# Feature sums of the norms in chained groups of four, modulation sums in chained pairs

## The chip, the cores and the metric

The kernel runs on one core of one Trainium2 chip. A core has engines that run side by side, each through its own queue in order: PE (matrix products, with a separate row PEld for the loading of weights), DVE, ACT and POOL (element-wise work), and SP, which issues most DMAs. The metric is device time in microseconds for one execution; lower is better. The time before is 3664.76 us, the median of three runs (3664.4 to 3665.83).

## The reference

Two post-norm layers over 1024 latent tokens and 256 context tokens of 1024 features, in float32. A layer modulates its input by vectors that come from a conditioning vector, projects it, runs three kinds of attention heads side by side, projects back, adds a gated residual and normalises; then a gated feed-forward with the same residual form. Cut to what the change touches:

```python
mod = (silu_c @ w_ada[l] + b_ada[l])[:, None, :]      # and the same for the context
sh1, sc1, g1, sh2, sc2, g2 = jnp.split(mod, 6, axis=-1)
x = layer_norm(DEEPNORM_ALPHA * x + g1 * (o @ w_out[l]), ln1_g[l], ln1_b[l])
x = layer_norm(DEEPNORM_ALPHA * x + g2 * swiglu(modulate(x, sh2, sc2), w_ffn_in[l], w_ffn_out[l]), ln2_g[l], ln2_b[l])

def layer_norm(x, g, b):
    mu = jnp.mean(x, axis=-1, keepdims=True)
    var = jnp.mean(jnp.square(x - mu), axis=-1, keepdims=True)
    return (x - mu) * lax.rsqrt(var + LN_EPS) * g + b
```

The context's stream goes through the same norms in the first layer only.

## The kernel before

Activations lie with features on the 128 partitions and tokens along the free axis, so 1024 features are eight tiles (`KT` = 8) of up to 1280 tokens. Tokens go in chunks of 512, 512 and, in the first layer, 256 (context). A projection (`mm3`, L278) is done in three PE passes on fp32r operands: weights and activations are split into a high and a low part (`whi` by ACT in L249, `wlo` mostly by POOL in L252), and hi·hi, hi·lo and lo·hi are added up in one PSUM bank. With eight feature tiles that is 24 products of 128x128 by 128x512 for 128 output features of one chunk. Each finished block of the output projection or of the feed-forward is added to the residual tile `z[kt]` by one DVE instruction (`ev_res`, L1198).

When all eight tiles of a chunk are there, `layer_norm` sums over the features. A sum over partitions is done on PE, by a product with a 128x32 tile of ones: `fsum` (L360 to L368) gives tile kt to the column quarter kt % 4 of PE, so that four partial sums stand on four blocks of 32 partitions of one PSUM bank, and tiles 4 to 7 are added onto those of 0 to 3. These are full fp32 products, which PE runs as two instructions each. ACT copies the bank out, another product brings the four quarters together and spreads the mean (L384). Then the mean is subtracted (tiles 0 to 3 on DVE, 4 to 7 on POOL; in the last norms 3 tiles on POOL), ACT squares each tile into a buffer `lnsq` (L395), `fsum` sums the squares, a few products and DVE steps give the reciprocal root, and the tiles are scaled and handed on: modulated and split for the next projection, scaled by the norm's own weights (POOL, L374), and stored. The buffers of the squares, of the mean's copy, of the bank's copy and of the modulated tiles are one pool of five (`t512`). There are ten such chunk norms: three and three in the first layer, two and two in the second, and each has two `fsum`, of eight products each.

While one chunk's norm runs, PE works at the projections of the next chunk, and the norm's products stand among them in PE's queue.

The conditioning vectors of the next parts are made beside the feed-forward and the projections: `ada_step` multiplies a 128x512 block of `w_ada` by the two conditioning columns on DVE (L177, L179), adds up eight such blocks in two accumulators, one for each column, and then two products with ones on two column quarters (L185) sum them over the partitions. Twenty such pairs are made.

The order of each engine's queue isn't the program's: a planner lays out all instructions when the kernel is built, by its own estimate of when each can start and by the order in which the program gives them. The kernel steers it with `gate(ins, after)`, an edge that only says that one instruction is issued after another, and `in_order`, which chains a list with such edges. Neither says that nothing else may come between. The sums of the softmax (`inverse_sums`, L498) and the spread of their inverses (`along`, L508) are chained in this way already. For the first norm of a layer, `hook` ties the 6th, 13th, 53rd, 58th and 73rd full-width projection product behind five steps of the norm: the last product of the first sum, the mean's, the last product of the second sum, the variance's and the root's.

Of the kernel before, what the change touches and what calls it, by code (L numbers as in the profile page):

```python
# [12 lines left out]
AF = mybir.ActivationFunctionType  # L13
ALU = mybir.AluOpType
# [8 lines left out]
KT = 8  # L23
# [30 lines left out]
def body(ctx: ExitStack, tc, xT, cT, w_ada, w_in, nbias, wa2, w_out, w_fi, w_fo, vecs, cc, consts, ropes, gmask, out):  # L54
    nc = tc.nc
    act, dve, pool, pe = nc.scalar, nc.vector, nc.gpsimd, nc.tensor
# [19 lines left out]
    def t512(name="t5"):  # L76
        return tmp.tile([P, 512], F32, tag="t5", name=name)
# [4 lines left out]
    def bank_x(name):  # L82
        return ps_x.tile([P, 512], F32, tag="x", name=name)

    def bank_a(name):
        return ps_a.tile([P, 512], F32, tag="a", name=name)
# [20 lines left out]
    ones = const.tile([P, 32], F32, name="ones")  # L107
# [10 lines left out]
    scc = const.tile([P, KT, 32], F32, name="scc")  # L118
# [21 lines left out]
    def ada_end(l, streams, ps, sel):  # L140
        sb = t512("adasb")
        act.copy(sb, ps)
        pv = bank_x("adav")
        for m in range(4):
            pe.matmul(pv[:, 4 * m:4 * m + 4], lhsT=sb[:, m * P:(m + 1) * P], rhs=sel, start=True, stop=True)
        for i, (part, half) in enumerate(streams):
            c0 = V_BADA + part * KT + half * 4
            dve.tensor_tensor(
                out=mod[l][:, part, half * 4:half * 4 + 4, :],
                in0=pv[:, 0:16].rearrange("p (m s) -> p m s", s=4)[:, :, 2 * i:2 * i + 2],  # L150
                in1=vec[l][:, c0:c0 + 4].unsqueeze(2).to_broadcast([P, 4, 2]), op=ALU.add)
# [13 lines left out]
    ada_todo, ada_run, ada_st = [], [], {}  # L165
# [6 lines left out]
    def ada_step(l, st, i, k, raw):  # L172
        if k == 0:
            ada_st["acc"] = [spool.tile([P, 512], F32, tag="hl", name="adacc") for _ in range(2)]
        for s_, a in enumerate(ada_st["acc"]):
            if k == 0:
                dve.tensor_scalar(a, raw, scc[:, k, s_:s_ + 1], None, ALU.mult)  # L177
            else:
                dve.scalar_tensor_tensor(out=a, in0=raw, scalar=scc[:, k, s_:s_ + 1], in1=a, op0=ALU.mult, op1=ALU.add)  # L179
        if k == KT - 1:  # L180
            if i == 0:
                ada_st["ps"] = bank_a("adaps")
            for s_, a in enumerate(ada_st["acc"]):
                q = 2 * i + s_
                pe.matmul(ada_st["ps"][32 * q:32 * q + 32, :], lhsT=ones[:, 0:32], rhs=a, start=True, stop=True)  # L185
            if i == 1:
                ada_end(l, st, ada_st["ps"], ident[:, 0:P:32])

# [115 lines left out]
    def hook(products_, offs):  # L304
        hk["c"] = 0
        hooks[:] = zip(offs, products_)
# [38 lines left out]
    def rsqrt_cols(src, n, eps, rows=P):  # L345
        v = small.tile([P, 20], F32, tag="rq_v", name="rq_v", bufs=2)
        y = small.tile([P, 20], F32, tag="rq_y", name="rq_y", bufs=2)
        t = small.tile([P, 20], F32, tag="rq_t", name="rq_t", bufs=2)
        v, y, t = v[:rows, :n], y[:rows, :n], t[:rows, :n]
        dve.tensor_scalar(v, src, eps, None, ALU.add)  # L350

        dve.tensor_scalar(y.bitcast(I32), v.bitcast(I32), -0.5, 1597463007.0, ALU.mult, ALU.add)
        for _ in range(3):
            dve.tensor_tensor(out=t, in0=y, in1=y, op=ALU.mult)
            dve.scalar_tensor_tensor(out=t, in0=t, scalar=-0.5, in1=v, op0=ALU.mult, op1=ALU.mult)
            dve.scalar_tensor_tensor(out=y, in0=t, scalar=1.5, in1=y, op0=ALU.add, op1=ALU.mult)
        return y


    def fsum(src, n):  # L360

        ps = bank_x("fs")
        for kt in range(KT):
            q = kt % 4
            ins = pe.matmul(ps[32 * q:32 * q + 32, :n], lhsT=ones[:, 0:32], rhs=src(kt), start=(kt < 4), stop=(kt >= 4))  # L365
        sb = t512("fssb")
        act.copy(sb[:, :n], ps[:, :n])
        return sb, ins  # L368
# [6 lines left out]

    NPOOL = 4
    NP3 = 3

    def layer_norm(z, t0, n, eps, consume, npool=NPOOL, offs=None):
        sl = slice(t0, t0 + n)  # L380
        nb = n // P
        sb, x1 = fsum(lambda kt: z[kt][:, sl], n)
        mps = bank_x("mean")
        x2 = pe.matmul(mps[:, :n], lhsT=onesm, rhs=sb[:, :n], start=True, stop=True)  # L384
        msb = t512("meansb")
        act.copy(msb[:, :n], mps[:, :n])
        for kt in range(KT):
            if kt >= KT - npool:
                pool.tensor_tensor(out=z[kt][:, sl], in0=z[kt][:, sl], in1=msb[:, :n], op=ALU.subtract)
            else:  # L390
                dve.tensor_tensor(out=z[kt][:, sl], in0=z[kt][:, sl], in1=mps[:, :n], op=ALU.subtract)

        def sq(kt):
            q = t512("lnsq")
            act.activation(q[:, :n], z[kt][:, sl], AF.Square)  # L395
            return q[:, :n]

        sb, x3 = fsum(sq, n)
        vps = bank_x("var")
        for b in range(nb):  # L400
            x4 = pe.matmul(vps[:, b:b + 1], lhsT=sb[:, b * P:(b + 1) * P], rhs=ones1, start=True, stop=True)
        y = rsqrt_cols(vps[:, :nb], nb, eps)
        rps = bank_x("rstd")
        for b in range(nb):
            x5 = pe.matmul(rps[:, b * P:(b + 1) * P], lhsT=y[:, b:b + 1].to_broadcast([P, P]), rhs=ident,
                           start=True, stop=True)
        if offs and n == 512:
            hook((x1, x2, x3, x4, x5), offs)
        rsb = t512("rstdsb")
        act.copy(rsb[:, :n], rps[:, :n])  # L410
        for kt in range(KT):
            if kt >= KT - npool:
                pool.tensor_tensor(out=z[kt][:, sl], in0=z[kt][:, sl], in1=rsb[:, :n], op=ALU.mult)
            else:
                dve.tensor_tensor(out=z[kt][:, sl], in0=z[kt][:, sl], in1=rps[:, :n], op=ALU.mult)
            consume(kt, sl)
# [24 lines left out]
    def gate(ins, after):  # L441

        if after is not None:
            tc.add_manual_dep(ins.ins, after.ins.name, NOSYNC, reason="buffers in order of use")
        return ins

    def in_order(inss):

        for a, b in zip(inss, inss[1:]):
            gate(b, a)  # L450
        return inss[-1]
# [80 lines left out]
    for l in range(NL):  # L532
# [35 lines left out]
        for e in range(2):  # L568
            ba = V[:, V_BA + e:V_BA + e + 1]
            for (t0, n) in FULL:  # L570
                ps = bank_q("zps")
# [4 lines left out]
        ins = [act.activation(a, a, AF.Exp, scale=-1.0) for a in dec][-1]  # L576
        ins = [gate(act.activation(a, a, AF.Ln, bias=one1), ins) for a in dec][-1]
# [45 lines left out]
        for p, ga, gb in abanks:  # L623
            dst, src, n = a_mm(p, ga, gb, gk, gq)
# [6 lines left out]
        for lev in range(6):  # L631
# [8 lines left out]
            for p, ga, gb in abanks:  # L640
                dst, src, n = a_mm(p, ga, gb, xk_, X)
# [81 lines left out]
        for p in range(2):  # L723
# [5 lines left out]
            for par in range(2):  # L729
                for g0, g1 in ((0, 8), (8, 10)):  # L730
                    pt = bank_q("inc")
                    for g in range(g0, g1):
                        for e in range(2):
                            for hh in range(2):
                                h, r0 = 2 * p + hh, 64 * e + 32 * hh
                                pe.matmul(pt[r0:r0 + 32, (g - g0) * 64:(g - g0 + 1) * 64],
                                          lhsT=kdt[e][64 * par:64 * par + 64, g * P + 32 * h:g * P + 32 * h + 32],
                                          rhs=vg(g)[64 * par:64 * par + 64, h * 64:(h + 1) * 64], start=True, stop=True)
# [13 lines left out]
            for i in range(1, NCH - 1):  # L752
                for e in range(2):
                    c, nx = order[e][i], order[e][i + 1]
# [3 lines left out]
                                             op0=ALU.mult, op1=ALU.add)  # L758
# [377 lines left out]
        sb = {"n": 0, "t": ps_s.tile([P, 2, 2, 512], F32, tag="s4", name="sT", bufs=1)}  # L1136
# [11 lines left out]
        for x, i in enumerate(PAIRS):  # L1148
            if x < 5:
                load(PAIRS[x + 1])  # L1150
            if x in (0, 2):
# [3 lines left out]
            a, na, places, skip = (  # L1155
                (some(PAIRS[1], None), steps_a[3], 22, 2), (), (some(PAIRS[3], None), steps_a[3] - half, 22, 2), (),
                (some(PAIRS[5], None), steps_a[3] - half, 22, 2), (iter(()), 0, 39, 0))[x] or (
                chain(some(PAIRS[x + 2], half), some(PAIRS[x + 1], None)), half + steps_a[0], 39, 3)
            live, tails = tails, []
            b = stage_b(i)  # L1160
            n = done = 0
# [22 lines left out]
        z = []  # L1184
# [9 lines left out]
        def ev_res(g, m):  # L1194
            def ev(ps, t0, n, c):
                s = 0 if t0 < SEQ else 1
                zz = z[m + c][:, t0:t0 + n]
                dve.scalar_tensor_tensor(out=zz, in0=ps[:, :n], scalar=g[:, m + c, s:s + 1], in1=zz,  # L1198
                                         op0=ALU.mult, op1=ALU.add)
            return ev  # L1200

        groups = GROUPS[l]
# [7 lines left out]
        for grp in groups:  # L1210
            for m in range(0 if grp[0][0] >= SEQ else 2, KT):
                dense(w_out[l, :, m * P:(m + 1) * P], oh_all, ol_all, grp, ev_res(ga1, m))
            for (t0, n) in grp:
                def consume(kt, sl, t0=t0, n=n):
                    modulate(u2h, u2l, z[kt][:, sl], kt, l, 1, t0, n, dve)
                    affine(AFF1, z[kt][:, sl], aGB[:, 0, kt:kt + 1], aGB[:, 1, kt:kt + 1])
# [51 lines left out]
        for grp in GROUPS[l]:  # L1268
# [4 lines left out]
            for (t0, n) in grp:  # L1273
                def consume2(kt, sl, t0=t0, n=n):
# [6 lines left out]
                    elif t0 < SEQ:  # L1281
                        nc.sync.dma_start(xs[kt * P:(kt + 1) * P, sl], z[kt][:, sl])
                layer_norm(z, t0, n, LN_EPS, consume2, NP3 if last else NPOOL)

# [99 lines left out]
```

## Time and profile before

| what | value |
|---|---|
| median of three runs | 3664.76 us (3664.4 to 3665.83) |
| the profiled execution's own time | 3658.13 us |
| its span, first to last instruction | 3656.3 us |
| PE busy | 3406.7 us, 93% |
| DVE, POOL, ACT busy | 1640.7, 1150.5, 920.8 us |
| mean granted clock of PE | 0.962 |
| products of `fsum` | 320 PE instructions |
| products of `ada_step` | 80 PE instructions |

A row of the timeline gives the start in us, the length in us, the engine, the line, the operation, output and inputs, the shape, and after x how many like instructions in a row were merged into it; in brackets stands idle time of the engine just before, and what ended it. Busy time of overlapping instructions is counted once. PE's products are pipelined, so that a product's length is more than its distance from the next one's start. Some matmul records can be missing.

### The profile page before, as it was taken

What the parts mean: (1) busy time and instruction counts of PE and PEld (TensorE: products, weight loads), DVE (VectorE), ACT (ScalarE), POOL (GpSimd) and SP (SyncE); (2) the same over time, 40 slices, a digit from 0 to 9 for tenths busy, and PEclk for the clock granted to TensorE, in tenths of its full rate; (3) what the DMA queues carried; (4) which work ended last, traced back from release to release, by engine and by line L of the source; (5) the groups of instructions that cost most, each with busy time, mean ns of one, the idle gap of its engine ahead of it and who ended that gap; (6) DMA issues with size and microseconds to landing.
All of it is one profiled execution on the core that took longest, in us unless ns stands there. A gap on an engine that the chain in (4) does not pass through costs nothing. (4 is left out here: it accounts for less than half of the span.)

```text
span 3656.3 us, 49289 instructions
## 1 busy us (share of the span) xinstructions
PE 3406.7 (93%) x20832; PEld 2519.1 (69%) x20832; DVE 1640.7 (45%) x2535; ACT 920.8 (25%) x1365; POOL 1150.5 (31%) x687
## 2 busy tenths in 40 slices
PE   6798987889999999999999988998889999999998
PEld 3576773434678888888886577773335688888875
DVE  2757725553444554554135473426552532222233
ACT  2213212333231111111113413212332311111114
POOL 1212214664451111111125521315662622222223
PEclk8798998999999999999999998998999999999999
DMA  5253330102221222222123221220103111111122
GB/s 173 62 153 96 127 118 28 64 1 81 70 61 63 92 86 72 78 84 67 37 68 98 77 87 56 73 104 32 58 1 107 46 50 52 47 52 48 48 73 86
DMA packets 287277, 262.94 MB, mean 72 GB/s; under 512 B 13840, under 2 KB 238416, under 8 KB 287056
## 3 DMA queue, kind: packets, MB, share of 16 engines
q1 hardware_dynamic: 287056, 259.80, 22.2%
q8 instruction: 163, 2.67, 0.3%
q14 instruction: 58, 0.48, 0.0%
HBM read 226.72 MB, written 33.03 MB: 71 GB/s over the span
## 5 line engine op out<-in xcount | busy, mean ns | idle before, releaser
L252 POOL TENSOR_TENSOR wlo<-wraw,whi 128x1024 fp32r<-128x1024 f32 (+3 forms) x228 | 505.0, 2216 | 1831.7 <-ACT whi L249 1773.9
L278 PE MATMUL mmps<-oh,whi 128*128 128x512 f32 (+2 forms) x2416 | 906.2, 376 | 18.8 <-ACT whi L249 7.2
L278 PE MATMUL mmps<-oh,wlo 128*128 128x512 f32 (+1 forms) x2416 | 903.2, 374 | 2.6 <-POOL wlo L252 2.6
L278 PE MATMUL mmps<-ol,whi 128*128 128x512 f32 (+1 forms) x2416 | 903.3, 374 | 1.9 <-DVE ol L231 1.9
L278 PEld LDWEIGHTS mmps<-oh,whi 128*128 128x128 f32 (+1 forms) x2416 | 458.2, 190 | 128.2 <-issue 20.9
L278 PEld LDWEIGHTS mmps<-oh,wlo 128*128 128x128 f32 x2416 | 457.5, 189 | 114.5 <-issue 24.7
L278 PEld LDWEIGHTS mmps<-ol,whi 128*128 128x128 f32 x2416 | 458.1, 190 | 97.4 <-issue 16.8
L249 ACT CAST whi<-wraw 128x1024 fp32r<-128x1024 f32 (+3 forms) x262 | 251.8, 962 | 968.2 <-PE mmps L278 907.9
L1229 DVE TENSOR_TENSOR sg<-mmps,sg 128x512 f32<-128x512 f32 (+1 forms) x110 | 70.1, 637 | 602.8 <-PE mmps L278 598.5
L278 PE MATMUL mmps<-hl,whi 128*128 128x512 f32 (+1 forms) x880 | 324.7, 369 | 1.0 <-DVE hl L1231 1.0
L278 PE MATMUL mmps<-hh,whi 128*128 128x512 f32 (+1 forms) x880 | 323.9, 371 | 0.0
L278 PE MATMUL mmps<-hh,wlo 128*128 128x512 f32 (+1 forms) x880 | 321.0, 369 | 0.0
L1198 DVE SCALAR_TENSOR_TENSOR z<-mmps,mod,z 128x512 f32<-128x512 f32 (+1 forms) x320 | 217.5, 694 | 196.6 <-PE mmps L278 195.9
L179 DVE SCALAR_TENSOR_TENSOR adacc<-adaw,scc,adacc 128x512 f32<-128x512 f32 x280 | 233.2, 877 | 95.3 <-DMA adaw<-in_w_ada_dram 95.0
L1069 POOL TENSOR_TENSOR gacc<-gacc,gpt 128x1024 f32<-128x1024 f32 x80 | 190.0, 2376 | 80.3 <-ACT gpt L1077 80.1
L957 DVE TENSOR_REDUCE m<-gs 128x2 f32<-128x1024 f32 (+1 forms) x150 | 154.8, 1032 | 106.6 <-PE gs L491 106.6
L278 PEld LDWEIGHTS mmps<-hh,whi 128*128 128x128 f32 x880 | 165.8, 189 | 41.4 <-issue 9.2
L278 PEld LDWEIGHTS mmps<-hh,wlo 128*128 128x128 f32 x880 | 165.5, 188 | 31.9 <-issue 2.5
L278 PEld LDWEIGHTS mmps<-hl,whi 128*128 128x128 f32 x880 | 165.9, 189 | 30.0 <-DVE hl L1231 1.2
L278 PE MATMUL mmps<-uh,whi 128*128 128x512 f32 (+3 forms) x408 | 155.1, 387 | 25.8 <-ACT uh L230 18.8
L1077 ACT ACTIVATE gpt<-sT 128x1024 f32<-128x1024 f32 x120 | 122.9, 1024 | 182.0 <-PE sT L483 166.8
L1231 DVE TENSOR_TENSOR hl<-sg,hh 128x512 fp32r<-128x512 f32 (+1 forms) x110 | 128.7, 1170 | 67.7 <-ACT hh L1230 67.6
(238 smaller groups left out, 4526.6 us busy)
## 6 DMA issues: line engine op xcount, KB each, us to landing
wraw<-in_w_fi_dram SPq DMA_DIRECT2D x106, 512.0 KB, 3.8
adaw<-in_w_ada_dram SPq DMA_DIRECT2D x160, 256.0 KB, 3.4
wraw<-in_w_fo_dram SPq DMA_DIRECT2D x60, 384.0 KB, 3.1
wraw<-in_w_in_dram SPq DMA_DIRECT2D x40, 512.0 KB, 4.1
wraw<-in_w_out_dram SPq DMA_DIRECT2D x36, 512.0 KB, 3.6
sp<-sphi SPq DMA_DIRECT2D x40, 256.0 KB, 2.0
sp<-splo SPq DMA_DIRECT2D x40, 256.0 KB, 2.1
adaw<-in_w_ada_dram SPq DMA_DIRECT2D x16, 512.0 KB, 7.5
```

What stands on the lines that cost most here:

```text
L179: dve.scalar_tensor_tensor(out=a, in0=raw, scalar=scc[:, k, s_:s_ + 1], in1=a, op0=ALU.mult, op1=ALU.add)
L249: act.copy(a[:, :m], rw)
L252: (dve if pace["lo"] and pace["w"] % pace["lo"] == 0 else pool).tensor_tensor(out=b[:, :m], in0=rw, in1=f(a[:, :m]), op=ALU.subtract)
L278: ins = pe.matmul(o, lhsT=lhs, rhs=rhs, start=st, stop=(k == nk - 1 and lhs is b))
L957: dve.tensor_reduce(out=m3[:, j, :, c], in_=ps[:, :, :n], axis=AX.X, op=ALU.max)
L1069: (dve if q and i == 5 else pool).tensor_tensor(out=acc[q], in0=prev if kb == 1 else acc[q], in1=pt, op=ALU.add)
L1077: act.activation(pt, ps, AF.Exp)
L1198: dve.scalar_tensor_tensor(out=zz, in0=ps[:, :n], scalar=g[:, m + c, s:s + 1], in1=zz, op0=ALU.mult, op1=ALU.add)
L1229: dve.tensor_tensor(out=sg[:, sl], in0=ps[:, :n], in1=sg[:, sl], op=ALU.mult)
L1231: dve.tensor_tensor(out=b_[:, sl], in0=sg[:, sl], in1=f(a_[:, sl]), op=ALU.subtract)
```

## The change

In `fsum`, the eight products become two groups of four, tiles 0 to 3 and tiles 4 to 7. Within a group the order is 3, 0, 1, 2 (and 7, 4, 5, 6), chained by `in_order`, and the first has an order edge to the instruction that made its input: the DVE instruction that last wrote that residual tile for this chunk (kept in `z_last`) or the ACT square. `fsum` returns the last product of the second group. In `ada_step` the two products are issued in reverse order, the second accumulator's first, with an order edge to its last DVE instruction, and chained. The products, their shapes, their quarters and their accumulation are the same.

```diff
@@ ada_step
-            for s_, a in enumerate(ada_st["acc"]):
-                q = 2 * i + s_
-                pe.matmul(ada_st["ps"][32 * q:32 * q + 32, :], lhsT=ones[:, 0:32], rhs=a, start=True, stop=True)
+            inss = [pe.matmul(ada_st["ps"][32 * q:32 * q + 32, :], lhsT=ones[:, 0:32], rhs=a, start=True, stop=True)
+                    for q, a in reversed(list(enumerate(ada_st["acc"], 2 * i)))]
+            gate(inss[0], ins)
+            in_order(inss)
...
@@ fsum
-        for kt in range(KT):
-            q = kt % 4
-            ins = pe.matmul(ps[32 * q:32 * q + 32, :n], lhsT=ones[:, 0:32], rhs=src(kt), start=(kt < 4), stop=(kt >= 4))
+        for k0 in (0, 4):
+            rhs, made = zip(*(src(k0 + q) for q in range(4)))
+            inss = [pe.matmul(ps[32 * q:32 * q + 32, :n], lhsT=ones[:, 0:32], rhs=rhs[q], start=(k0 == 0), stop=(k0 == 4))
+                    for q in (3, 0, 1, 2)]
+
+            gate(inss[0], made[3])
+            ins = in_order(inss)
...
@@ layer_norm
-        sb, x1 = fsum(lambda kt: z[kt][:, sl], n)
+        sb, x1 = fsum(lambda kt: (z[kt][:, sl], z_last.get((kt, t0))), n)
...
-            act.activation(q[:, :n], z[kt][:, sl], AF.Square)
-            return q[:, :n]
+            return q[:, :n], act.activation(q[:, :n], z[kt][:, sl], AF.Square)
...
@@ ev_res
-                dve.scalar_tensor_tensor(out=zz, in0=ps[:, :n], scalar=g[:, m + c, s:s + 1], in1=zz,
-                                         op0=ALU.mult, op1=ALU.add)
+                z_last[m + c, t0] = dve.scalar_tensor_tensor(out=zz, in0=ps[:, :n], scalar=g[:, m + c, s:s + 1],
+                                                             in1=zz, op0=ALU.mult, op1=ALU.add)
```

More of the change, by code (lines that the diff above doesn't have):

```diff
@@ L176, in ada_step @@
             if k == 0:
-                dve.tensor_scalar(a, raw, scc[:, k, s_:s_ + 1], None, ALU.mult)
+                ins = dve.tensor_scalar(a, raw, scc[:, k, s_:s_ + 1], None, ALU.mult)
             else:
-                dve.scalar_tensor_tensor(out=a, in0=raw, scalar=scc[:, k, s_:s_ + 1], in1=a, op0=ALU.mult, op1=ALU.add)
+                ins = dve.scalar_tensor_tensor(out=a, in0=raw, scalar=scc[:, k, s_:s_ + 1], in1=a, op0=ALU.mult,
+                                               op1=ALU.add)
         if k == KT - 1:
@@ L377, in body @@
     NP3 = 3
+    z_last = {}
     def layer_norm(z, t0, n, eps, consume, npool=NPOOL, offs=None):
```

## The prediction

> **What bounds the kernel now.** I began with the page: spans, busy shares, then the chain that ended last by line.
>
> ```profile
> span 3656.3 us, 49289 instructions
> ...
> PE 3406.7 (93%) x20832; PEld 2519.1 (69%) x20832; DVE 1640.7 (45%) x2535; ACT 920.8 (25%) x1365; POOL 1150.5 (31%) x687
> ```
>
> PE is the engine that is full; the next is at 45%. The change touches only the stages around the norms, so I then asked for the busy time in those stretches, where the columns are PE, PEld, DVE, ACT, POOL, the granted clock and DMA.
>
> ```profile
> 905.00:960.00 55.00, 55.00 (x225) 37.48 (x224) 15.97 (x18) 9.79 (x11) 12.20 (x5) 1.00 0.36 113
> 985.00:1045.00 60.00, 54.81 (x306) 39.79 (x305) 35.21 (x53) 22.56 (x32) 42.84 (x26) 0.94 0.30 88
> 1980.00:2010.00 30.00, 28.79 (x144) 18.63 (x144) 22.49 (x26) 12.67 (x21) 23.45 (x16) 1.00 0.56 176
> 2010.00:2045.00 35.00, 31.39 (x187) 20.95 (x186) 25.18 (x45) 14.44 (x23) 23.13 (x16) 0.95 0.40 125
> 2870.00:2910.00 40.00, 38.15 (x165) 25.26 (x164) 19.25 (x36) 16.32 (x25) 25.07 (x18) 1.00 0.16 46
> ```
>
> While the first chunk's norm runs, PE is busy the whole stretch (55.00 of 55.00) and everybody else idles half the time: time taken off PE there is time taken off the kernel. In the second chunk's stretches PE still leads, but POOL comes near: 42.84 of 60, 23.45 of 30, 23.13 of 35 and 25.07 of 40 us.
>
> Next, the instructions of the sums themselves (PE only): count, ns min/median/max.
>
> ```profile
> L365 PE MATMUL fs<-z,ones x160: 379/592/636, 917.1 to 3630.9; 128*32 128x512 f32 x128, 128*32 128x256 f32 x32
> L365 PE MATMUL fs<-lnsq,ones x160: 379/592/1062, 968.5 to 3640.4; 128*32 128x512 f32 x128, 128*32 128x256 f32 x32
> its engine sat idle before it (us, times) until:
>   ACT lnsq L395: 3.5, 3
>   DVE z L1198: 2.7, 2
> ```
>
> Ten norms with two sums of eight products are 160 products, recorded as 320 instructions: every fp32 product is two PE instructions. A busy sum of these is no cost, since they overlap. The cost is what they do to the stream of projection products, and that is in PE's timeline.
>
> ```profile
> 936.12 0.39 PE L278 MATMUL mmps<-ol,whi 128*128 128x512 f32 x1
> 936.44 1.04 PE L365 MATMUL fs<-z,ones 128*32 128x512 f32 x2
> 937.42 0.50 PE L278 MATMUL mmps<-oh,wlo 128*128 128x512 f32 x1
> 937.76 0.39 PE L278 MATMUL mmps<-oh,whi 128*128 128x512 f32 x1
> 937.99 0.39 PE L278 MATMUL mmps<-ol,whi 128*128 128x512 f32 x1
> ...
> 2852.76 0.39 PE L278 MATMUL mmps<-oh,whi 128*128 128x512 f32 x1
> 2853.08 1.06 PE L365 MATMUL fs<-lnsq,ones 128*32 128x512 f32 x8
> 2854.08 0.50 PE L278 MATMUL mmps<-ol,whi 128*128 128x512 f32 x1
> 2854.42 0.39 PE L278 MATMUL mmps<-oh,wlo 128*128 128x512 f32 x1
> ```
>
> This is the heart of it. In the undisturbed stream a projection product starts about every 0.225 us (937.76, 937.99). One sum product alone (x2) holds the stream from 936.12 to 937.76, 1.64 us for two starts: it costs 1.64 − 2 × 0.225 = **1.19 us**. Four products on the four column quarters (x8) hold it from 2852.76 to 2854.42, 1.66 us, a cost of **1.21 us**. So the price is per interruption, not per product: three of four products ride free when they stand together.
>
> How often is the stream interrupted? I counted the runs of sum products in PE's timeline, from the first of the 512-column chunks to the last that has a stream around it:
>
> ```profile
> 917.07 1.05 PE L365 MATMUL fs<-z,ones 128*32 128x512 f32 x4
> ...
> 3597.19 1.04 PE L365 MATMUL fs<-lnsq,ones 128*32 128x512 f32 x2
> ```
>
> Seven chunks, in order of time. Sums of the values: 7, 4, 7, 8, 6, 4, 6 runs, together 42. Sums of the squares: 6, 6, 6, 5, 5, 4, 5, together 37 (one row of ten instructions counted as two). That is **79 interruptions for 112 products**. With groups of four it would be 7 × 4 = **28**.
>
> **The change part by part.** No instruction is added, removed or altered in shape; only PE's order is tied down. The edge from the last made input to the first product of a group repeats a dependence the data has anyway: nothing by itself. The DMAs and the other engines keep their work. The hooks of the first norms still tie projection products 6, 13, 53, 58 and 73 behind the same five steps, two of which are the last product of a sum.
>
> *Do chained products stand together?* The chain orders them but forbids nothing in between. Chains that this kernel already has, and sum products that were ready together:
>
> ```profile
> 608.09 1.06 PE L498 MATMUL sums<-acc,ones 128*32 128x512 f32 x8 [0.58 <-ACT NM L469]
> 887.98 1.05 PE L498 MATMUL sums<-gacc,ones 128*32 128x512 f32 x4 [0.30 <-POOL gacc L1069]
> ...
> 891.10 1.05 PE L498 MATMUL sums<-gacc,ones 128*32 128x512 f32 x4
> ...
> 908.68 1.08 PE L508 MATMUL rb<-ri,cst 128*64 128x512 f32 x4
> ...
> 990.44 1.06 PE L365 MATMUL fs<-z,ones 128*32 128x512 f32 x6
> ```
>
> The chained four at 608.09 and the chained pair at 908.68, inside the projection stream, are one run each. The chain at 887.98 broke in two, and it starts with products whose inputs were ready early: that is what starting with the last made input avoids. At 990.44 three products that were ready went in one run, unchained. So I take one run per group for the squares. For the sums of values I allow five groups broken once, since most of their runs hold a single product beside a stream that could have gone on.
>
> *Squares:* 37 − 14 = 23 runs × 1.19 = 27.4 us. *Values:* 42 − 14 − 5 = 23 × 1.19 = 27.4 us; between 0 (no group holds) and 28 × 1.19 = 33.3 us (all hold).
>
> [...]
>
> *The 256-column chunks* run in 17 pieces; 8 would be left.
>
> ```profile
> 1067.44 0.64 PE L365 MATMUL fs<-lnsq,ones 128*32 128x256 f32 x8
> ...
> 2034.96 1.06 PE L365 MATMUL fs<-z,ones 128*32 128x256 f32 x2 [2.30 <-DVE z L1198]
> ```
>
> At 0.64 us and the successor's delay as above (0.34 − 0.225 = 0.11), 9 × 0.75 = 6.8 us; but PE stands waiting beside them (2.30 us at 2034.96), so I take 3, between 0 and 6.8.
>
> *The modulation sums* are pairs and mostly stand together already; four of twenty pairs are split like this one.
>
> ```profile
> 1720.93 1.05 PE L185 MATMUL adaps<-adacc,ones 128*32 128x512 f32 x2
> ...
> 1722.57 1.04 PE L185 MATMUL adaps<-adacc,ones 128*32 128x512 f32 x2
> ...
>   DVE adacc L179: 12.2, 5
> ```
>
> Four runs × 1.19 = 4.8 us. The last line (idle time of PE before these products) says that five of them also wait 2.4 us each for the accumulation on DVE; a pair tied to the later input waits for the same end, so nothing changes there. I take 4.
>
> *What PE's gain meets.* Of the 51 runs saved among the 512 columns, 19 are in second chunks (values 4+8+4 − 6, squares 6+5+4 − 6). There POOL subtracts, multiplies and scales the first chunk's and its own rows, and cuts weights in between. POOL's four stretches above sum to 114.5 busy of 165 us; PE faster by 19 × 1.19 = 22.6 us makes that 80%, and its work comes in blocks, with PE waiting for weights behind it:
>
> ```profile
> PE mmps L278 <- ACT whi L249: 7.2, 2, 4.5
> ```
>
> I count half of the 22.6 us as lost there: −11, between 0 and −22.6.
>
> *Squares and their buffers.* Before, each square's tile came free after its own product; after, four must wait for the group. There are five tiles of that kind, one holding the mean:
>
> ```profile
> 965.55 1.14 ACT L395 ACTIVATE lnsq<-z 128x512 f32<-128x512 f32 x2
> 967.77 0.63 ACT L395 ACTIVATE lnsq<-z 128x512 f32<-128x512 f32 x1 [1.08 <-POOL z L389]
> 969.61 0.63 ACT L395 ACTIVATE lnsq<-z 128x512 f32<-128x512 f32 x1 [1.20 <-PE fs L365]
> ```
>
> ACT already waits for POOL to let go of the mean and then for PE to let go of a square. The second four squares will come as a block of 4 × 0.62 = 2.5 us behind the first group. Inside the stream PE has other products meanwhile: nothing. Behind it is POOL's weight cutting only if ACT's conversions queue behind those squares, up to 2.5 us once per norm. In the last norm nothing covers it:
>
> ```profile
> 3634.72 3.08 ACT L395 ACTIVATE lnsq<-z 128x512 f32<-128x512 f32 x5 [0.75 <-DVE z L391]
> ...
> 3635.40 5.16 PE L365 MATMUL fs<-lnsq,ones 128*32 128x512 f32 x15 [2.06 <-ACT lnsq L395]
> 3639.80 1.19 PE L365 MATMUL fs<-lnsq,ones 128*32 128x512 f32 x3
> ```
>
> Four squares end at 3634.72 + 4 × 0.616 = 3637.2, the group at 3638.3, four more squares at 3640.8, the second group at 3642.0; today it is 3639.80 + 1.19 = 3641.0. One microsecond lost, or none if the fifth tile is free early.
>
> **The sum:** 27.4 + 27.4 + 3 + 4 − 11 − 1 = 49.8, say 50 us. The profiled execution took 3658.1 us itself (1.8 around its span); it would take 3608. It lies 6.6 us below the median of the three runs, 3664.8, so I predict 3664.8 − 50 = **3615 us**.
>
> **The rivals.** *Nothing is lost:* all groups hold and POOL does not bind: 27.4 + 33.3 + 6.8 + 4.8 = 72, 3593 us. For it: PE waits little in any stage. Against: the 4.5 us wait for weights lies in just such a stretch.
>
> *The groups of values break:* the planner that lays out PE's order fills them into gaps one at a time, as it does now at 936.44. Then squares 27.4, modulation 4 and 1 of the small chunks remain, less 4 on POOL: 28 us, 3637. For it: single products 6.7 us apart in the first chunk. Against: the three at 990.44.
>
> *The change does not do what it says:* projection products slip into all chains and the count of runs stays: 3665 us. Against it are all the chained runs shown.
>
> *Slower, by a blocked queue:* the planner sets a group where it believes the last input made; if the chip makes it later, the group's first product, and everything behind it on PE, waits. Today an early product of the group would have used that time. There are 36 groups outside the last chunk; at 2.4 us each, as the modulation sums wait now, 88 us are lost and 50 gained: 3703. It decides from a mean wait of 50 / 36 = 1.4 us. Against it: the sum products waited only 3.5 us in three places and 2.7 in two. [...]
>
> **How the numbers follow.** Forecast 62%, nothing lost 12%, values break 15%, no effect 5%, blocked queue 6%. A measurement of this kernel tells 0.2%, some 7 us, from no change. Faster is the sum of the first three, 0.89; the same 0.05; slower 0.06. The range runs from 3592, where nothing is lost, to 3642, a little past the broken groups.
>
> **What would show it.** Right: runs of sum products fall from 79 to about 28 to 35, nearly all x8 at 1.06; PE's busy time falls by about 50 us with the same 20832 instructions; projection products after a run still start 0.34 us apart once. POOL wrong: the wait for weights beside norms stays below 10 us, and the time is nearer 3593. Values wrong: x2 rows between projection products in their sums. The last norm's squares should end 1 us later relative to its mean. The prediction is wrong if runs fall to 28 and the time does not follow, or if idle time of PE ahead of sum products passes 20 us.

## The result, and the profile after

The changed kernel takes **3628.73 us** (median of four runs, 3624.58 to 3631.78) beside 3664.58 us for the kernel before (median of four): a ratio of **0.9906, interval [0.9894, 0.9919]**, or 36 us less. The forecast was 3615 us, with a range of 3592 to 3642. One slow run of all those behind this text, 9133.75 us of the kernel with less work for POOL, is left out.

The profiled execution took 3630.86 us, against 3658.13 us for that of before. That is 27 us, so the two profiles show somewhat less than the medians. The page of the changed kernel begins:

```profile
span 3629.1 us, 49276 instructions
...
PE 3349.5 (92%) x20832; PEld 2518.5 (69%) x20832; DVE 1645.6 (45%) x2535; ACT 920.7 (25%) x1365; POOL 1147.1 (32%) x687
```

PE does the same 20832 instructions in 3406.7 − 3349.5 = **57.2 us less busy time**. But the span fell only by 3656.3 − 3629.1 = 27.2 us: PE's idle time rose from 249.6 to 279.6 us, by **30.0 us**. The rest of this text is about these two numbers.

First, the sum products. The rows of PE's timeline in the changed kernel show a group of values inside the stream, two groups of squares with all that stood between them, and a group of values that broke:

```profile
959.26 1.07 PE L367 MATMUL fs<-z,ones 128*32 128x512 f32 x8
...
2823.93 0.39 PE L280 MATMUL mmps<-ol,whi 128*128 128x512 f32 x1
2824.25 1.07 PE L367 MATMUL fs<-lnsq,ones 128*32 128x512 f32 x8
2825.24 0.50 PE L280 MATMUL mmps<-oh,wlo 128*128 128x512 f32 x1
2825.58 0.40 PE L280 MATMUL mmps<-oh,whi 128*128 128x512 f32 x1
2827.05 1.06 PE L367 MATMUL fs<-lnsq,ones 128*32 128x512 f32 x8 [1.07 <-ACT lnsq L402]
...
2840.58 1.06 PE L367 MATMUL fs<-z,ones 128*32 128x512 f32 x6
...
2847.24 1.05 PE L367 MATMUL fs<-z,ones 128*32 128x512 f32 x2
```

The group at 2824.25 holds the stream from 2823.93 to 2825.58, 1.65 us for four products, where 1.66 us was read before. Counted as in the prediction, the seven chunks of 512 columns that have a stream around them now have 17 runs of values (3, 3, 2, 2, 2, 3, 2) and 14 of squares: 31 in place of 79. Over the whole kernel, with a run counted as one as long as PE does nothing else in between, it is 41 runs in place of 97.

New is the 1.07 us at 2827.05. PE has two projection products between the two groups of squares and then stands. The view of the instructions that write the sums (PE only) gives the total of such waits; the ACT row there was 3.5 us in three places before:

```profile
L367 PE MATMUL fs<-lnsq,ones x160: 379/592/1062, 971.6 to 3610.9; 128*32 128x512 f32 x128, 128*32 128x256 f32 x32
its engine sat idle before it (us, times) until:
  ACT lnsq L402: 12.1, 7
```

Five of the seven are inside the stream, 5.9 us together; the other two are in the last norm.

Second, where PE idles. Busy time by stretch (PE, PEld, DVE, ACT, POOL, clock, DMA) of the kernel before; the stretches are the 900 us ahead of the first norm, and then the four stages with norms, the last one up to the end:

```profile
0.00:900.00 900.00, 766.83 (x6232) 506.51 (x6233) 496.48 (x815) 262.16 (x404) 300.87 (x195) 0.91 0.27 87
900.00:1085.00 185.00, 176.72 (x815) 123.10 (x814) 80.26 (x127) 57.16 (x84) 87.78 (x53) 0.96 0.29 89
1900.00:2070.00 170.00, 164.66 (x749) 106.09 (x748) 82.55 (x132) 58.93 (x94) 82.96 (x53) 0.99 0.31 95
2790.00:2905.00 115.00, 112.38 (x467) 75.00 (x467) 43.90 (x73) 37.04 (x51) 55.35 (x32) 1.00 0.23 67
3600.00:3656.30 56.30, 40.44 (x180) 26.87 (x178) 22.35 (x49) 23.59 (x35) 16.78 (x12) 0.88 0.27 96
```

The same of the changed kernel, whose stages lie somewhat earlier:

```profile
0.00:900.00 900.00, 761.41 (x6206) 503.14 (x6207) 496.78 (x813) 261.90 (x403) 301.56 (x195) 0.91 0.26 85
900.00:1085.00 185.00, 172.32 (x880) 130.92 (x880) 87.01 (x139) 59.77 (x91) 91.63 (x59) 0.96 0.31 96
1900.00:2060.00 160.00, 146.08 (x809) 108.39 (x809) 87.93 (x137) 58.92 (x98) 86.31 (x59) 0.96 0.32 99
2785.00:2900.00 115.00, 107.28 (x485) 78.75 (x484) 55.52 (x90) 40.63 (x59) 66.60 (x42) 0.97 0.20 58
3570.00:3629.10 59.10, 37.30 (x173) 25.96 (x171) 21.91 (x49) 23.33 (x35) 16.77 (x12) 0.80 0.25 91
```

PE's idle time is the length less the first number. It goes from 133.2 to 138.6 ahead of the norms (+5.4), from 8.3 to 12.7 (+4.4), from 5.3 to 13.9 (+8.6), from 2.6 to 7.7 (+5.1), and in the last stage from 15.9 to 21.8 (+5.9). These five make 29.4 of the 30.0.

The third column from the end says one thing more. In the second and the third stage with norms the granted clock of PE falls from 0.99 to 0.96 and from 1.00 to 0.97, so some of PE's products there are longer than before. By these rows that is at most 0.04 × 160 − 0.01 × 170 + 0.03 × 115, some 8 us of PE's busy time, an estimate; the 57.2 us are what is left after it. The prediction has no term for it; the last section shows one such place.

The waits of PE in the stage with the largest rise, 1900 to 2060 us of the changed kernel (total us, times, longest):

```profile
PE mmps L280 <- ACT oh L232: 3.0, 1, 3.0
PE mmps L280 <- DVE wlo L254: 2.7, 1, 2.7
PE mmps L280 <- DVE ol L233: 2.5, 2, 2.0
PE mmps L280 <- POOL wlo L254: 2.2, 3, 1.0
PE mmps L280 <- ACT whi L251: 1.4, 1, 1.4
...
PE fs L367 <- ACT lnsq L402: 0.8, 1, 0.8
```

The largest of the stage at 900 us, and the two largest of the stage at 2785 us:

```profile
PE mmps L280 <- ACT whi L251: 9.7, 4, 4.5
...
PE mmps L280 <- POOL wlo L254: 2.9, 1, 2.9
PE fs L367 <- ACT lnsq L402: 2.8, 2, 1.7
```

The projection products wait for weights and activations, from three engines. Over the three stages PE waits 18.9 us for weights (`whi`, `wlo`), 7.7 for activations (`oh`, `ol`, `hl`) and 5.9 for squares; in the kernel before it is 9.8, 1.0 and 1.4 us. In the middle stage alone, the kernel before waits 2.3 us for a residual tile, 1.4 for squares, 1.0 for the feed-forward's low half and 0.5 for a copy; none is for weights.

### The profile page after: what moved, and what is told of

Read it like the earlier page. It is cut to its first block, busy times and chain, and to the rows that moved or that the text cites. A ratio compares the mean times of both kernels' runs of the same rounds, so it can differ in the third digit from the quotient of the medians.

```text
span 3629.1 us, 49276 instructions
## 1 busy us (share of the span) xinstructions
PE 3349.5 (92%) x20832; PEld 2518.5 (69%) x20832; DVE 1645.6 (45%) x2535; ACT 920.7 (25%) x1365; POOL 1147.1 (32%) x687
## 5 line engine op out<-in xcount | busy, mean ns | idle before, releaser
L280 PE MATMUL mmps<-oh,wlo 128*128 128x512 f32 (+2 forms) x2416 | 905.2, 375 | 8.0 <-POOL wlo L254 5.3
L280 PE MATMUL mmps<-ol,whi 128*128 128x512 f32 (+2 forms) x2416 | 903.2, 374 | 4.4 <-DVE ol L233 4.4
L280 PEld LDWEIGHTS mmps<-oh,wlo 128*128 128x128 f32 (+1 forms) x2416 | 459.5, 190 | 111.5 <-issue 14.6
L280 PEld LDWEIGHTS mmps<-ol,whi 128*128 128x128 f32 (+1 forms) x2416 | 460.1, 190 | 93.3 <-issue 9.2
L280 PEld LDWEIGHTS mmps<-hl,whi 128*128 128x128 f32 x880 | 165.9, 189 | 29.4 <-issue 0.8
```

The source lines that it names most:

```text
L280: ins = pe.matmul(o, lhsT=lhs, rhs=rhs, start=st, stop=(k == nk - 1 and lhs is b))
```

## The experiments

Kernels that were run together share the runs of the kernel before: 3662.99 us for the modulation's two and for the values and the squares alone, 3660.16 for the pairs, the two with more tiles after the change and the one with less work for POOL, and 3662.59 for the other four. Ratios go against those.

### The modulation part, without and alone

The change with the old modulation sums, and the modulation's edit alone:

```diff
@@ without it: ada_step as before
-            inss = [pe.matmul(ada_st["ps"][32 * q:32 * q + 32, :], lhsT=ones[:, 0:32], rhs=a, start=True, stop=True)
-                    for q, a in reversed(list(enumerate(ada_st["acc"], 2 * i)))]
-            gate(inss[0], ins)
-            in_order(inss)
+            for s_, a in enumerate(ada_st["acc"]):
+                q = 2 * i + s_
+                pe.matmul(ada_st["ps"][32 * q:32 * q + 32, :], lhsT=ones[:, 0:32], rhs=a, start=True, stop=True)
@@ alone: fsum as before, and its callers with it
-        for k0 in (0, 4):
-            rhs, made = zip(*(src(k0 + q) for q in range(4)))
...
-            gate(inss[0], made[3])
-            ins = in_order(inss)
+        for kt in range(KT):
+            q = kt % 4
+            ins = pe.matmul(ps[32 * q:32 * q + 32, :n], lhsT=ones[:, 0:32], rhs=src(kt), start=(kt < 4), stop=(kt >= 4))
```

> The groups of four in the norms, the modulation sums as before. Theory: the modulation part costs about 5 us, since the order of the first 900 us was laid out anew around it and PE waits 5.2 us more for the accumulators there; this kernel then takes 36 + 5 = 41 us less than before, about 3624 us. Rival: the 5 us come from the norms' chains through the planner, and the modulation part gains up to 4 us as predicted; then this kernel is no faster than the change, 3629 us or up to 4 us more.

> The chained pairs of the modulation sums, the norms as before. Theory: about 5 us slower than before, 3669 us, with PE waiting some 16 us for the accumulators in the first 900 us instead of 10.6. Rival (the prediction's term): four pairs no longer split, 4 us faster, 3661 us.

Without it: 3631.97 us, ratio 0.9918 [0.9904, 0.9932]. Alone: 3657.11 us, ratio 0.9987 [0.9978, 0.9996]. So the modulation part takes off 6 us when it stands alone. Taken out of the change it makes 3 us by the medians, with overlapping intervals, so that way of asking shows only that it costs nothing. The forecast of 4 stands, and that it costs 5 us falls.

I had suspected a cost because PE's wait for the accumulators ahead of the first norm rose. The waits of PE in the first 900 us, the changed kernel:

```profile
PE adaps L184 <- DVE adacc L179: 15.8, 4, 6.1
```

It was 10.6 us in four places before. In the ten other kernels of this study with the same modulation part it is 9.3 to 15.5 us, and 9.9 and 11.6 in the two without it. So the changed kernel's profile lies at the upper end of what is seen, and these 5.4 us of its idle time can't be put down to the norms' groups. Which of the planner's choices moves it was not tried.

### Values alone, squares alone

`fsum` gets a switch, and one of its two calls goes back to single products (the modulation stays as changed):

```diff
-        sb, x3 = fsum(sq, n)
+        sb, x3 = fsum(sq, n, False)        # values alone
...
-        sb, x1 = fsum(lambda kt: (z[kt][:, sl], z_last.get((kt, t0))), n)
+        sb, x1 = fsum(lambda kt: (z[kt][:, sl], z_last.get((kt, t0))), n, False)   # squares alone
```

> Chained groups for the sums of the values, the sums of the squares as before, the modulation pairs chained. Theory: about 25 of 42 interruptions fewer at 1.19 us, 30 us, less 4 us at POOL's work in the second chunks and 5 us for the modulation part: 21 us less than before, 3643 us. Rival: the groups of values bring little, since their products filled gaps, and nearly all of the 36 us come from the squares: 3660 us.

> Chained groups for the sums of the squares, the sums of the values as before, the modulation pairs chained. Theory: 23 interruptions fewer, 27 us, of which some 10 us are lost to second groups that wait for their squares (five tiles), 4 us in the last norm and 5 us to the modulation part: 8 us less than before, 3656 us. Rival: those waits only stand where PE would have waited anyway, and the squares keep all 27 us less 5: 3642 us.

Values alone: 3643.6 us, ratio 0.995 [0.9936, 0.9964]. Squares alone: 3647.4 us, 0.9959 [0.9947, 0.9972]. Less the 6 us of the modulation alone, the values bring some 14 us and the squares some 10. With the modulation's 6 that makes 29 us, where the change itself takes off 34 (by the ratio) to 36; where the difference comes from was not followed. PE's busy time falls by 30.3 and 28.5 us (from 3406.7 to 3376.4 and 3378.2), 27.6 and 25.8 without the 2.7 that the modulation alone takes off. So both halves save what the sum of the prediction gave them in busy time, 27.4 each, and **both** give half of it or more back as idle time. What eats the gain is not in the squares alone.

### Pairs in place of fours

```diff
-        for k0 in (0, 4):
-            rhs, made = zip(*(src(k0 + q) for q in range(4)))
+        for k0 in range(0, KT, 2):
+            rhs, made = zip(*(src(k0 + j) for j in range(2)))
...
-            gate(inss[0], made[3])
+            gate(inss[0], made[1])
```

> Chained pairs in the norms instead of groups of four. If an interruption costs 1.19 us whatever stands in it, about 56 of them instead of 31 put 25 x 1.19 = 30 us back on PE, of which some 10 us fill waits that the groups of four have: 20 us slower than the change, 3649 us. Rival, that the order alone (last made first) and not the number of runs makes the gain: within 5 us of the change.

3639.01 us, ratio 0.9941 [0.9929, 0.9954]: 10 us slower than the change by the medians, between what the two theories gave. The profile says why it is between. The pairs stand in 60 runs in place of 41, and PE is busy for 3376.3 us, 26.8 us more than in the change: 1.4 us for each of the 19 runs more, somewhat above the 1.19 that the prediction priced. But the span of 3638.8 us leaves 262.5 us idle, 17.1 us less than in the change. So the slower PE waited less here.

### The first made input first

The chain stays, but it runs 0, 1, 2, 3, and its first product is tied to the first made input:

```diff
-                    for q in (3, 0, 1, 2)]
+                    for q in (0, 1, 2, 3)]
-            gate(inss[0], made[3])
+            gate(inss[0], made[0])
```

> The changed kernel, with the first made of four put first in the chain in place of the last made; the three behind it follow in the order in which they are made. Theory A (the wait of the chain's first product for the last made input is what keeps four products together): PE starts on the first and can wait inside the run, and a projection product slips in there for at least half of the 31 runs, at 1.19 us, so 10 to 25 us slower than the change, 3639 to 3654 us. Rival B (products of one chain stay together on PE whichever comes first, and a wait inside a run costs PE the same as one ahead of it): within 4 us of the change, 3625 to 3633 us.

3656.25 us, ratio 0.9985 [0.9976, 0.9994]: no better than the modulation part alone, and 27 us slower than the change, a little more than the theory of the wait allowed. Its timeline, PE's rows, first norm; the values come by themselves again:

```profile
936.57 1.05 PE L367 MATMUL fs<-z,ones 128*32 128x512 f32 x2
```

There are 97 runs, as many as before, and PE is busy for 3403.8 us. So a chain does not group anything. It says only which comes first, and the planner fills the time to the next input with projection products as it did without a chain. **The gain in the norms hangs on one thing: that the product that can start last is first in the chain.** The theory that a chain stays together whichever comes first falls. Whether the edge on that first product would do without the chain behind it was not run.

### More tiles for the squares

Three kernels: a sixth tile in the pool; the squares of tiles 4 to 7 in other pools' tiles; and, as a control, the sixth tile in the kernel before.

```diff
-    tmp = ctx.enter_context(tc.tile_pool(name="tmp", bufs=5))
+    tmp = ctx.enter_context(tc.tile_pool(name="tmp", bufs=6))      # the change, and before as control
...
-            q = t512("lnsq")
+            if kt < 4:
+                q = t512("lnsq")
+            else:
+                q = (apool if kt < 6 else spool).tile([P, 512], F32, tag="ada" if kt < 6 else "hl", name="lnsq")
```

> The change, with six tiles in the pool of the squares instead of five. Theory A, that second groups wait for tiles: PE's waits for squares fall from 12 us to about half, some 4 us faster than the change, 3625 us. Theory B, that the gain is lost to weights and modulated rows that come late beside the norms: no difference, 3629 us.

> The change, with the squares of tiles 4 to 7 in four tiles of their own (those of the modulation's blocks and accumulators, idle during most norms). Theory A: no second group waits for a tile; PE's waits for squares fall by 6 us or more and the last norm by 2 us, 8 us faster than the change, 3621 us. Theory B: no difference beyond the last norm's 2 us, 3627 us.

> The kernel before, with nothing changed but a sixth tile in the pool of intermediate tiles. Theory A (the sixth tile helped the changed kernel through the groups of squares, which ask for four tiles at once): the kernel before takes its squares one by one and gains at most 2 us, so about 3658 to 3662 us beside 3660. Theory B (a sixth tile helps any kernel of this kind, since low halves and residuals draw on the same pool): it gains the same 11 us or so, about 3649 us, and the tiles say nothing on the change.

The change with six tiles: **3617.81 us**, ratio 0.9881 [0.9868, 0.9895]. With other pools' tiles: 3622.05 us, 0.9898 [0.9883, 0.9913]. The kernel before with six tiles: 3676.46 us, **1.0038** [1.0026, 1.0051], 14 us slower. So a sixth tile is no gift to any kernel; it helps through the groups. (Where the control loses: 10.2 us in PE's busy time, with 100 runs of sum products in place of 97, and 8.2 us idle, 2.0 of them in the first layer's second norms and 3.7 between these and the next layer's. Why the planner scatters the sums more was not followed.)

The second group of squares with six tiles, PE's row in the same place as 2827.05 above:

```profile
2818.03 1.06 PE L367 MATMUL fs<-lnsq,ones 128*32 128x512 f32 x8 [0.56 <-ACT lnsq L402]
```

The five waits inside the stream are 1.08, 1.22, 0.81, 1.07 and 1.74 us with five tiles and 0.56, 0.48, 0.81, 0.56 and 1.22 with six. From five tiles to six that is only 2.3 us of the 11 by which the medians differ (9 by the ratios). With other pools' tiles two such waits are left, of 0.24 and 0.81 us. Between the first and the last of ACT's copies of the sums in each stage, the six-tile kernel's idle time is 2.5 us lower than the change's in the first three stages, and 0.6 lower from the last stage's first copy to the end. Another 1.7 us lie between the second stage and the third, and 7.6 ahead of the first norm, where the groups play no part and where the profiles differ anyway. So the tile pool is shown as a cause of some 3 us of the idle time. The rest of the 11 is measured, but not explained.

### Less work for POOL

```diff
-LN_LO = 3
+LN_LO = 2        # of the low halves cut beside norms, more go to DVE
```

> The change, with every second low half of the weights beside the norms made on DVE instead of every third. Theory B with POOL as the late one: PE's waits for weights beside the norms fall, 5 us faster than the change, 3624 us. Theory A, or DVE as the late one: no gain, 3629 us, or up to 5 us slower, since DVE then holds the norm's own steps and the modulated rows longer.

3633.2 us, ratio 0.9925 [0.9911, 0.9938]. POOL's busy time falls by 35 us (1147.1 to 1112.2) and DVE's rises by 20, and the kernel gains nothing. Busy time by stretch of this kernel:

```profile
900.00:1085.00 185.00, 174.82 (x908) 134.75 (x908) 94.33 (x152) 61.82 (x97) 88.03 (x59) 0.99 0.31 95
...
2785.00:2900.00 115.00, 102.91 (x453) 74.43 (x454) 58.62 (x90) 39.18 (x58) 57.56 (x37) 0.96 0.20 58
```

The first stage's idle time falls by 2.5 us, the third one's rises by 4.4; the second one's stays, 13.8 us beside 13.9. In the third PE waits (2785 to 2915 us):

```profile
PE mmps L280 <- POOL wlo L254: 4.0, 1, 4.0
PE mmps L280 <- DVE wlo L254: 3.4, 3, 1.9
```

The wait moves between engines. So POOL by itself is not the bound that the prediction made it.

### The last norm's squares one by one

`fsum` is chained everywhere but for the squares of the last chunk; the second kernel has six tiles as well.

```diff
-        sb, x3 = fsum(sq, n)
+        sb, x3 = fsum(sq, n, npool != NP3 or t0 == 0)
```

> The changed kernel, with the squares of the very last chunk taken one by one again, as before. Theory A (behind the last projection product there is nothing to interrupt, so the chain there only makes PE wait for four squares): the end comes 3 to 4 us earlier than in the changed kernel, about 3625 us beside 3629, with the last rstd to the end unchanged. Rival B (the slower products there, 1.94 us for a group, come from the idling and not from the chain): the change in the end is under 1.5 us, about 3628 us.

> The changed kernel with a sixth intermediate tile and the last chunk's squares taken one by one: 11 us and 3 to 4 us less than the change if the two add up, about 3614 us. Rival: the sixth tile already shortens the end (from the mean's product to the rstd product 15.6 us with six tiles, 16.1 with five, 12.8 before), so that only about 3 us of the two overlap or less; then 3615 to 3616 us. If the loose squares bring nothing, 3618 us, as with the sixth tile alone.

With five tiles: 3624.34 us, ratio 0.9897 [0.9883, 0.991]. With six: **3617.25 us**, 0.9879 [0.9864, 0.9894]. PE's rows at the end of the changed kernel:

```profile
3600.80 1.12 PE L391 MATMUL mean<-fssb,ones 128*128 128x512 f32 x2 [0.73 <-ACT fssb L373]
3605.84 1.94 PE L367 MATMUL fs<-lnsq,ones 128*32 128x512 f32 x8 [3.91 <-ACT lnsq L402]
3610.03 1.94 PE L367 MATMUL fs<-lnsq,ones 128*32 128x512 f32 x8 [2.26 <-ACT lnsq L402]
3612.67 1.87 PE L407 MATMUL var<-ones,fssb 128*128 128x1 f32 x8 [0.70 <-ACT fssb L373]
3616.86 2.05 PE L411 MATMUL rstd<-cst,rq_y 128*128 128x128 f32 x8 [2.32 <-DVE rq_y L358]
```

The same with five tiles and loose squares:

```profile
3595.13 1.12 PE L396 MATMUL mean<-fssb,ones 128*128 128x512 f32 x2 [0.73 <-ACT fssb L378]
3598.31 5.05 PE L376 MATMUL fs<-lnsq,ones 128*32 128x512 f32 x16 [2.06 <-ACT lnsq L407]
3604.04 1.05 PE L412 MATMUL var<-ones,fssb 128*128 128x1 f32 x8 [0.67 <-ACT fssb L378]
3607.42 2.04 PE L416 MATMUL rstd<-cst,rq_y 128*128 128x128 f32 x8 [2.32 <-DVE rq_y L358]
```

And of the kernel before:

```profile
3632.22 1.12 PE L384 MATMUL mean<-fssb,ones 128*128 128x512 f32 x2 [0.68 <-ACT fssb L367]
...
3645.04 1.13 PE L405 MATMUL rstd<-cst,rq_y 128*128 128x128 f32 x8 [2.32 <-DVE rq_y L356]
```

From the start of the mean's product to that of the root's it is 16.06 us with groups, 12.29 without, and 12.82 before. So the chain costs 3.8 us at the end, as expected, and the ratio's 3.3 us less agree in size, though its interval overlaps the change's. With six tiles the loose squares are worth nothing that the medians show (3617.25 beside 3617.81), while the trace of that kernel shows the same 12.3 us; of the cases written down it is nearest to the one in which they bring nothing. Both six-tile kernels are faster than the change, by 11 us of the medians, though their intervals just touch its own: they end at 0.9895 and 0.9894, where the change's begins.

## Why the prediction was right, and where its sum was off

The direction, the mechanism and the range held. The likeliest case was named as 3615 us, 14 us too good. By steps:

*The price is per interruption: right.* The groups of 512 columns in the stream take 1.06 to 1.07 us, but for one of 1.93 at a granted clock of 0.50, and the one shown holds the stream for 1.65 us. Runs fell to 31, within the 28 to 35 that were to show it, and the instructions are the same 20832. The sum of what PE saves was 27.4 + 27.4 + 3 + 4 = 61.8 us; measured are 57.2, with the longer products of the lower clock in them. The pairs, at 1.4 us for each further run, agree roughly.

*Chained products stand together: right for the reason given.* The prediction said that starting with the last made input avoids the break seen at 887.98. The kernel with the first made first shows that this is no refinement: without it the gain is gone. Three groups of values broke, not five; none of the squares in the stream.

*The modulation: right.* 4 forecast, 6 measured alone, 3 within the noise taken out of the change.

*What PE's gain meets: the mechanism right, the engine wrong, the size near.* I took 11 us, on POOL, in second chunks. In the stages with norms PE's idle time rose by 4.4 + 8.6 + 5.1 = 18.1 us. The waits for squares are 4.5 of these (5.9 us in place of 1.4); some 14 us remain in which a faster PE meets work of other engines that does not come faster. The wait for weights beside norms is 18.9 us, not below 10, so the sign that was to show the step wrong did not come. But the waits are for ACT, DVE and POOL in turn, and giving 35 us of POOL's work to DVE moved them and brought nothing. That the values alone lose about as much as the squares alone, and the pairs less than the fours, fits it. No run slowed or sped all three suppliers at once, so it is the best reading of the waits rather than a shown cause. The clock that falls beside these waits (0.99 to 0.96 and 1.00 to 0.97) is a further loss that the step did not have, at most some 8 us by the estimate above, and no run separates it from them.

*Squares and their buffers: the step that failed.* "Inside the stream PE has other products meanwhile: nothing." It has two, and then waits: the second group can't be squared until the first frees its tiles, and the `hook`, which the prediction itself described, holds the 53rd projection product behind the last product of the second group; counted in PE's rows, the product behind the group at 2827.05 is that one. The waits for squares in the stream rose by 4.5 us, and a sixth tile takes 2.3 of them off. No run moved the hook.

*The last norm: the size failed.* One microsecond was forecast, 3.2 measured between the mean and the root (16.06 − 12.82), 3.8 against the loose squares. The first squares group must wait for four squares, 3.91 us where 2.06 was. The prediction had that wait, and it had the tiles free only after the whole group; but the group that it took for 1.1 us lasted 1.94, as ACT's row of the changed kernel shows, which starts the second four squares 1.95 us after the group's start. The second group and the variance's products were longer too (1.94 and 1.87 us), below. The prediction took durations from a busy PE for a place where PE idles.

```profile
3607.79 2.19 ACT L402 ACTIVATE lnsq<-z 128x512 f32<-128x512 f32 x4 [2.00 <-PE fs L367]
```

So the sum, on the profiles: 57.2 saved, 18.1 lost beside norms, 5.9 at the end, 5.4 ahead of the norms where the change has little hand, 0.6 elsewhere: 27.2. By the medians 36. The forecast's 50 was 61.8 − 12; had the losses of 24 been known it would have been 38 us.

The blocked queue, the rival on the slower side, is what these waits are in small: 12.1 us for squares in place of 3.5. It would have decided from a mean wait of 1.4 us at each of 36 groups; the five waits in the stream have 1.2 us on average, and the other groups have next to none. With the values' 2.6 us PE's wait ahead of sum products is 14.7 us in all, below the 20 that were to show the prediction wrong.

## What to carry to other kernels

A chain of order edges groups nothing by itself under such a planner: put the product whose input comes last at its head, and the rest rides along at next to no cost (here one product alone held the stream for 1.64 us, a group of four for 1.65). Before grouping, count the buffers that the group's inputs hold at once, and leave single what stands at the end of the kernel with no stream to protect. And a saving on a full engine is worth its busy time only up to the pace of those that feed it: here 57 us of busy time became 27 in the profiles and 36 by the medians, and the idle time by stage shows how much each stage gave back.

## What the runs showed of the hardware

**Behind some waits PE's granted clock was 0.50, behind others 1.00.** A group that takes 1.06 us in the stream took 1.94 at 3605.84, after 3.91 us of idling, with the clock at 0.50 (3605.8 to 3608 us), and the next ones stayed slow (1.94, 1.87). Inside the stream a group took 1.93 behind a wait of 2.94 us. Two rows of the timeline of the changed kernel, and two stretches, in which the granted clock is the third column from the end:

```profile
2857.06 0.50 PE L280 MATMUL mmps<-oh,wlo 128*128 128x512 f32 x1 [2.94 <-POOL wlo L254]
...
2857.96 1.93 PE L367 MATMUL fs<-z,ones 128*32 128x512 f32 x8
...
2858.00:2861.00 3.00, 3.00 (x12) 1.15 (x12) 0.00 (x0) 0.59 (x1) 1.34 (x1) 0.50 0.59 175
...
3612.00:3629.00 17.00, 3.92 (x16) 3.56 (x16) 4.87 (x16) 6.92 (x10) 3.74 (x3) 0.50 0.33 123
```

And stretches of the kernel before, just behind the 2.06 us of idling at 3635.40, and at its end:

```profile
3636.00:3638.00 2.00, 2.00 (x8) 0.69 (x8) 1.07 (x2) 1.80 (x3) 1.79 (x2) 0.50 0.00 0
...
3640.00:3656.00 16.00, 3.17 (x19) 2.01 (x18) 4.87 (x16) 6.92 (x10) 3.73 (x3) 0.69 0.35 131
```

The clock is 0.50 over the last 17 us of the changed kernel, against 0.69 over the last 16 before. In the kernel with loose squares the same 2.06 us of idling left the clock at 1.00 (3597 to 3606 us), and the variance's eight took 1.05 there, beside 1.87 at 0.50. So the length of the wait alone does not decide, and what does was not tested.

**A DVE subtraction of two tiles took 1.23 us by itself and 1.88 to 3.20 beside four of POOL's.** DVE's and POOL's rows of the changed kernel:

```profile
953.70 1.23 DVE L254 TENSOR_TENSOR wlo<-wraw,whi 128x1024 fp32r<-128x1024 f32 x1
...
1987.27 3.20 DVE L254 TENSOR_TENSOR wlo<-wraw,whi 128x1024 fp32r<-128x1024 f32 x1 [1.55 <-ACT whi L251]
```

```profile
1987.02 2.36 POOL L254 TENSOR_TENSOR wlo<-wraw,whi 128x1024 fp32r<-128x1024 f32 x1
```

The same cut of a weight's low half took 1.23 us by itself and 3.20 while POOL ran one of its own from 1987.02 to 1989.38; PE then waited 2.7 us for it, the row "DVE wlo" of its waits. Beside POOL's subtraction of the mean, also of two tiles, it took 1.88 to 2.30 us in three places (1016.24, 1924.17, 2819.38). Beside POOL's scaling of one tile it took 1.21 in four (1001.85, 1048.26, 2015.51, 2847.09). At 922.48, where POOL's own subtraction began 0.82 us after DVE's, it took 1.22. So not everything that POOL ran beside it went with a longer time, and why four places did was not tested.
